# A new order of the FFN products, their sums, their weight buffers and the first loads in a two-layer trunk kernel

## The chip, the cores and the metric

The kernel runs on one core of a Trainium2 chip. The metric is device time in microseconds (us) of one execution. TensorE (PE) multiplies; VectorE (DVE), ScalarE (ACT) and GpSimd (POOL) do everything else on tiles of 128 partitions; SyncE (SP) only issues loads. Each engine works through its own list of instructions in order, and waits at an instruction until what that one needs has happened.

## The reference

Two layers, one sequence of 512 positions, width 1024, float32. Each layer is a mixer (layer 0: gated spatial mixing beside latent attention; layer 1: retention) and then a SwiGLU FFN of width 2816, each behind an RMSNorm and added to the residual `x`:

```
x = x + mixer(rmsnorm(x, g1))
h = rmsnorm(x, g2)
x = x + (silu(h @ w_gate) * (h @ w_up)) @ w_down      # 1024 -> 2816 -> 1024
```

The change touches the start of layer 0 and the two FFNs.

## The kernel before, in words

Activations are held transposed, in eight chunks of 128 features by 512 positions. A float32 product is three matmuls on a high and a low part of each side (hi·hi, hi·lo, lo·hi). Weights come as a "tape": `Tape.load` takes the next block of 128x1024 (512 KB), loads it over SP's queue into a buffer `w_raw` (L211), lets ACT round it to `w_hi` (L214) and DVE take the rest, `w_lo` (L215). Four blocks are kept split ahead of the product that uses them (DEPTH = 4). Activations are split the same way: `h_hi` by ACT (L356) and `h_lo` by DVE (L357) for the normed input, `a_hi` (L281) and `a_lo` (L282) for the FFN's inner values.

In the FFN the 22 blocks of 128 inner features are 11 pairs. Pair 0 is computed plainly ("whole"). Of each other pair, gate and up are got together by a Strassen-like scheme with seven products instead of eight. A product is 24 matmuls with a moving side of 256. Their names are A11, S1, S2, A12, S3, A22 and S4, after the weight blocks that they use. Three of the blocks are loaded plainly. S1 and S3 are sums of two blocks: a plain load (L211), then a second load on POOL's queue that adds into the same buffer (L213). S2 = A11 + S1 and S4 = A12 + S2 are made by DVE, in place in the first buffer (L199). S2, S3 and A22 go on accumulating in the PSUM bank `ps_x` that A11 began. Before each of S2, S3 and A22 starts, ACT has to copy the bank's state so far into a tile J: `take` (L894). `add` (L897, DVE) brings the other banks in. `finish` makes the inner values from a pair of rows: multiply by the norm's factor R (L877), Silu on ACT (L878), multiply by the other half (L879), split. After pairs 3, 7 and 10 the finished blocks go through w_down ("down", L923 and L924 add to `x`).

`ffn_steps` lists the products in the order in which TensorE does them. The order on the other engines is made by the tile framework's scheduler when the program is built; on the chip it is fixed. Loads of the tape wait until a buffer of the `raw` pool is free: 3 buffers in most of the kernel, 7 in the FFN.

Of the kernel before, what the change touches and what calls it, by code (L numbers as in the profile page):

```python
# [38 lines left out]
def ffn_steps():  # L39


    steps = [("whole", 0)]
    for p0, p1 in FF_PARTS:
        for p in range(max(p0, 1), p1):
            if p == 1:
                steps.append(("A11", p))
            steps += [("S1", p), ("S2", p), ("A12", p), ("S3", p)]
            if p + 1 < PAIRS:
                steps.append(("A11", p + 1))
            steps += [("A22", p), ("S4", p)]  # L50
        steps.append(("down", (p0, p1)))
    return steps


def tape_spec():

    out = []  # L60
    c = lambda a, n: np.arange(a, a + n)

    def load(name, k0, nk, cols, streams=False):
        key = (name, k0, int(cols[0]))
        block = (key, [(name, k0 + k, cols) for k in range(nk)], streams)
        out.append((key, ("load", block), nk, len(cols)))

    for m in range(2):
        load("even_w_in", 0, 8, c(1408 + 128 * m, 128))
    for m in range(3):  # L70
        load("even_w_in", 0, 8, c(1024 + 128 * m, 128))
    for k in range(0, 8, 2):
        load("even_w_in", k, 2, c(512, 512), True)
    head = np.arange(8)[:, None] * 128
    load("mla_w_ukv", 0, 2, (head + np.arange(64)[None]).ravel(), True)
    load("mla_w_ukv", 0, 2, (head + 64 + np.arange(64)[None]).ravel(), True)
    for k in range(3):
        load("mla_w_uq", k, 1, c(0, 768), True)
    for m in range(4):
        load("even_w_in", 0, 8, c(128 * m, 128))  # L80
    for k in (0, 4):
        for m in range(4):
            load("even_w_out", k, 4, c(256 * m, 256))

    def ffn(layer):
        gate, up, down = (f"ffn_w_{n}{layer}" for n in ("gate", "up", "down"))

        def block(i, j, p):

            cols = c(256 * p + 128 * i, 128)  # L90
            pieces = [(w, 2 * k + j, cols) for k in range(KD // 2) for w in (gate, up)]
            return ((gate, p, i, j), pieces, False)

        for name, p in ffn_steps():
            key = (layer, p, name)
            if name == "whole":
                for m in (2 * p, 2 * p + 1):
                    for w in (gate, up):
                        load(w, 0, 8, c(128 * m, 128))
                continue  # L100
            if name == "down":
                k0, k1 = 2 * p[0], 2 * p[1]
                for m in range(8):
                    load(down, k0, k1 - k0, c(128 * m, 128))
                continue
            how = {
                "A11": ("load", block(0, 0, p)),
                "A12": ("load", block(0, 1, p)),
                "A22": ("load", block(1, 1, p)),
                "S1": ("sum", block(1, 0, p), block(1, 1, p)),  # L110
                "S3": ("sum", block(1, 0, p), block(0, 0, p)),
                "S2": ("add", (layer, p, "A11"), (layer, p, "S1")),
                "S4": ("add", (layer, p, "A12"), (layer, p, "S2")),
            }[name]
            out.append((key, how, KD // 2, 256))

    def odd_out(h):
        for m in range(4):
            load("odd_w_out", 4 * h, 4, c(256 * m, 256))

    ffn(0)
    for h in range(RH):
        for base in (0, 1024):
            for m in range(2):
                load("odd_w_in", 0, 8, c(base + 256 * h + 128 * m, 128))
        for k in range(0, 8, 2):
            load("odd_w_in", k, 2, c(2048 + 512 * h, 512), True)
        for m in range(4):
            load("odd_w_in", 0, 8, c(4096 + 512 * h + 128 * m, 128))
        if h:  # L130
            odd_out(h - 1)
    odd_out(RH - 1)
    ffn(1)
    return out


def tape_blocks():

    blocks, at = {}, 0
    for _, how, _, _ in tape_spec():  # L140
        for b in how[1:] if how[0] != "add" else ():
            if b[0] not in blocks:
                blocks[b[0]] = (b, at)
                at += P * sum(len(cols) for _, _, cols in b[1])
    return blocks
# [31 lines left out]
class Tape:  # L177
# [13 lines left out]
    def load(self, pieces=1):  # L191
        key, how, nk, n = self.spec[len(self.made)]
        w = nk * n
        nc = self.nc
        hi = self.parts.tile([P, CHUNK], F32R, name="w_hi")
        lo = self.parts.tile([P, CHUNK], F32R, name="w_lo")
        if how[0] == "add":
            t = self.raws.pop(how[1])
            nc.vector.tensor_tensor(t[:, :w], t[:, :w], self.raws[how[2]][:, :w], op=ALU.add)  # L199
        else:  # L200
            t = self.raw.tile([P, CHUNK], F32, name="w_raw")
        self.raws[key] = t
        src = []
        if how[0] != "add":
            for b in how[1:]:
                at = self.begin[b[0]]
                src.append(self.wtape[at : at + P * w].rearrange("(p w) -> p w", p=P))
        for i in range(pieces):
            c = slice(i * w // pieces, (i + 1) * w // pieces)
            if src:  # L210
                nc.sync.dma_start(out=t[:, c], in_=src[0][:, c])  # L211
            for more in src[1:]:
                nc.gpsimd.dma_start(out=t[:, c], in_=more[:, c], accum_op=ALU.add)  # L213
            nc.scalar.copy(hi[:, c], t[:, c])  # L214
            nc.vector.tensor_tensor(  # L215
                lo[:, c], t[:, c], hi[:, c].bitcast(F32), op=ALU.subtract
            )
        view = lambda x: x[:, :w].rearrange("p (k n) -> p k n", k=nk)
        self.made.append((view(hi), view(lo)))

# [15 lines left out]
def trunk_kernel(ctx: ExitStack, tc: tile.TileContext, a: dict, out: bass.AP):  # L236
# [21 lines left out]
    def new_raw(stack, bufs):  # L258
        tape.raw = stack.enter_context(tc.tile_pool(name="raw", bufs=bufs))

    gains = const.tile([P, 4, KD], F32, name="gains")
    nc.scalar.dma_start(out=gains, in_=a["gains"])
    x = [res.tile([P, S], F32, name=f"x{k}") for k in range(KD)]
    ident = const.tile([P, P], F32, name="ident")
    make_identity(nc, ident)
    ones = const.tile([P, P], F32, name="ones")
    nc.vector.memset(ones, 1.0)
    mhalf = const.tile([P, 1], F32, name="mhalf")
    nc.vector.memset(mhalf, -0.5)
# [157 lines left out]
    with ExitStack() as e:  # L427
        new_raw(e, 3)
        h = []
        for k in range(KD):  # L430
            nc.sync.dma_start(out=x[k], in_=a["xT"][k * P : (k + 1) * P, :])
            if k == 0:
                tape.load(pieces=4)
            h.append(scaled_parts(0, k))
        tape.load(pieces=2)
        tape.ahead()
        new_tmp(e)
# [5 lines left out]
        for k in range(KD):  # L443
# [3 lines left out]
        cgain = ev.tile([P, 5], F32, name="cgain")  # L447
        qkg = ev.tile([P, 2, QK0], F32, name="qkg")
        rope0 = ea.tile([P, NT, 2, ROPE], F32, name="rope0")
        nc.gpsimd.dma_start(out=cgain, in_=a["lat_gT"])  # L450
        wk = ea.tile([P, KD, ROPE], F32, name="wk")
        nc.gpsimd.dma_start(out=wk, in_=a["kpe_w"])
        nc.gpsimd.dma_start(
            out=qkg, in_=a["qk_g"].rearrange("(o j) f -> o j f", o=1).broadcast_to([P, 2, QK0])
        )
        nc.gpsimd.dma_start(out=rope0, in_=a["rope0"])
        nc.gpsimd.dma_start(out=vgain, in_=a["gm_gT"])


        lat, latp = [], []  # L460
# [351 lines left out]
    def ffn(h, ss, which):  # L812
# [5 lines left out]


        with ExitStack() as e:  # L820
            new_raw(e, 7)
            fp = e.enter_context(tc.tile_pool(name="fp", bufs=1, reuse_waits="tile"))
            fp2 = e.enter_context(tc.tile_pool(name="fp2", bufs=2, reuse_waits="tile"))
            q = S // 2
# [109 lines left out]
            own = lambda t: t  # L934
            for name, p in ffn_steps():
                if name == "A11":
                    xs, rows = bank("ps_x"), [wide(), None]
                    products(xs, name, True)
                    take(rows[0], 0, xs)
                    following = (xs, rows)  # L940
                    if p == 1:
                        R = ss.rows(norm)
                        for m in range(2):
                            finish(m, undone(whole[m][0]), undone(whole[m][1]), plain)
# [7 lines left out]
                if name == "A12":  # L952
                    ws = bank("ps_w")
                    products(ws, name, True)
                    add(rows[0], 0, ws)
                if name == "S3":
                    products(xs, name, False)
                    rows[1] = wide()
                    take(rows[1], 1, xs, -1.0)
                    add(rows[1], 1, vs, ALU.subtract)  # L960
                    here = (xs, rows)
                if name == "A22":
                    xs, rows = here
                    products(xs, name, False)
                    take(rows[1], 0, xs, -1.0)
                    finish(2 * p + 1, rows[1][:, :S], rows[1][:, S:], own)
# [229 lines left out]
```

## Time and profile before

| | us |
|---|---|
| median of 3 runs (lowest, highest) | 1239.76 (1239.07, 1240.69) |
| the profiled execution | 1239.42 |
| its span, first to last instruction | 1237.6 |
| PE busy in the span | 1219.7 (99%) |
| DVE busy | 853.4 (69%) |
| ACT busy | 563.0 (45%) |
| POOL busy | 85.5 (7%) |
| mean granted TensorE clock | 0.997 |

PE, DVE, ACT and POOL are the compute engines; the busy time of PE is the sum of its matmuls, whose ends are modelled. What lies between the span and the execution's time, 1.8 us, is outside the program's instructions.

### The profile page before, as it was taken

The numbers are of one execution on the slowest core, as the hardware profiler recorded it, in microseconds if no ns is written. First come the engines' busy times: TensorE is split into PE (matmuls) and PEld (weight loads), VectorE is DVE, ScalarE is ACT, GpSimd is POOL, SyncE is SP. The second block draws the span as 40 slices with busy tenths as digits, with TensorE's granted clock in tenths as the row PEclk, the third lists the DMA queues.
The fourth block names the chain that finished last, engine by engine and source line by source line (L and its number), as shares of the span: only waits on it lengthen the run. The fifth ranks groups of instructions, "written<-read, shape, count | busy, mean of one in ns | idle before, by whom it ended". The sixth has DMA issues, their size and how long they took to land. (4 is left out here: it accounts for less than half of the span.)

```text
span 1237.6 us, 18425 instructions
## 1 busy us (share of the span) xinstructions
PE 1219.7 (99%) x7464; PEld 1106.2 (89%) x7464; DVE 853.4 (69%) x1226; ACT 563.0 (45%) x811; POOL 85.5 (7%) x89
## 2 busy tenths in 40 slices
PE   8999999999999999999999999999998999999998
PEld 6897778898999899888888888888888989998997
DVE  6597748986597577955474574574778756875774
ACT  5465746653366245534242242242466524652551
POOL 2062000100000000000000000000010000000000
PEclk9999999999999999999999999999999999999999
DMA  7223115655575556132231332332265565754631
GB/s 233 83 75 120 35 34 171 168 173 153 139 193 172 144 144 177 72 119 102 69 102 68 103 102 69 102 103 68 86 180 161 171 151 139 204 162 128 166 108 68
DMA packets 44980, 155.32 MB, mean 125 GB/s; under 512 B 5232, under 2 KB 5776, under 8 KB 44768
## 3 DMA queue, kind: packets, MB, share of 16 engines
q1 hardware_dynamic: 38304, 130.70, 31.7%
q0 software_dynamic: 6448, 23.45, 10.7%
q8 instruction: 58, 0.95, 0.3%
q14 instruction: 26, 0.21, 0.0%
q10 hardware_dynamic: 144, 0.02, 0.0%
HBM read 152.04 MB, written 2.10 MB: 125 GB/s over the span
## 5 line engine op out<-in xcount | busy, mean ns | idle before, releaser
L214 ACT CAST w_hi<-w_raw 128x1024 fp32r<-128x1024 f32 (+3 forms) x290 | 294.3, 1021 | 479.9 <-PE ps_mm L288 230.2
L215 DVE TENSOR_TENSOR w_lo<-w_raw,w_hi 128x1024 fp32r<-128x1024 f32 (+3 forms) x290 | 345.3, 1198 | 128.2 <-ACT w_hi L214 127.7
L287 PE MATMUL ps_mm<-h_hi,w_hi 128*128 128x512 f32 x456 | 175.4, 385 | 3.7 <-ACT h_hi L356 3.5
L288 PE MATMUL ps_mm<-h_lo,w_hi 128*128 128x512 f32 x456 | 173.9, 382 | 0.7 <-DVE h_lo L357 0.6
L289 PE MATMUL ps_mm<-h_hi,w_lo 128*128 128x512 f32 x456 | 173.5, 381 | 0.0
L865 PE MATMUL ps_x<-t_hi,w_hi 128*128 128x256 f32 x480 | 133.6, 278 | 6.7 <-ACT J L894 6.6
L287 PE MATMUL ps_mm<-a_hi,w_hi 128*128 128x512 f32 x352 | 133.5, 380 | 0.3 <-ACT a_hi L281 0.3
L289 PE MATMUL ps_mm<-a_hi,w_lo 128*128 128x512 f32 x352 | 133.6, 379 | 0.0
L288 PE MATMUL ps_mm<-a_lo,w_hi 128*128 128x512 f32 x352 | 133.6, 379 | 0.0
L865 PE MATMUL ps_x<-t_lo,w_hi 128*128 128x256 f32 x480 | 132.8, 277 | 0.0
L865 PE MATMUL ps_x<-t_hi,w_lo 128*128 128x256 f32 x480 | 132.8, 277 | 0.0
L287 PEld LDWEIGHTS ps_mm<-h_hi,w_hi 128*128 128x128 f32 x456 | 86.7, 190 | 16.5 <-ACT h_hi L356 3.8
L865 PEld LDWEIGHTS ps_x<-t_hi,w_hi 128*128 128x128 f32 x480 | 92.9, 194 | 8.2 <-ACT J L894 8.2
L288 PEld LDWEIGHTS ps_mm<-h_lo,w_hi 128*128 128x128 f32 x456 | 86.6, 190 | 14.2 <-DVE h_lo L357 2.4
L289 PEld LDWEIGHTS ps_mm<-h_hi,w_lo 128*128 128x128 f32 x456 | 86.6, 190 | 12.3 <-DVE w_lo L215 0.5
L865 PEld LDWEIGHTS ps_x<-t_lo,w_hi 128*128 128x128 f32 x480 | 92.9, 194 | 0.0
L865 PEld LDWEIGHTS ps_x<-t_hi,w_lo 128*128 128x128 f32 x480 | 92.9, 193 | 0.0
L213 POOL DMA_DIRECT2D w_raw<-in_wtape x40 | 34.7, 869 | 629.4 <-DMA w_raw<-in_wtape 249.2
L287 PEld LDWEIGHTS ps_mm<-a_hi,w_hi 128*128 128x128 f32 x352 | 66.5, 189 | 10.2 <-ACT a_hi L281 1.1
L289 PEld LDWEIGHTS ps_mm<-a_hi,w_lo 128*128 128x128 f32 x352 | 66.6, 189 | 9.3
L288 PEld LDWEIGHTS ps_mm<-a_lo,w_hi 128*128 128x128 f32 x352 | 66.7, 189 | 9.1
L923 DVE TENSOR_TENSOR t<-ps_mm,R 128x512 f32<-128x512 f32 x48 | 33.1, 689 | 59.3 <-PE ps_mm L289 59.2
(226 smaller groups left out, 2595.6 us busy)
## 6 DMA issues: line engine op xcount, KB each, us to landing
w_raw<-in_wtape SPq DMA_DIRECT2D x225, 512.0 KB, 3.5
w_raw<-in_wtape POOLq DMA_DIRECT2D x40, 512.0 KB, 5.8
w_raw<-in_wtape SPq DMA_DIRECT2D x19, 384.0 KB, 3.2
x<-in_xT SPq DMA_DIRECT2D x8, 256.0 KB, 6.4
out_T<-x SPq DMA_DIRECT2D x8, 256.0 KB, 2.0
decay<-in_decay POOLq DMA_DIRECT2D x1, 1024.0 KB, 7.2
w_raw<-in_wtape SPq DMA_DIRECT2D x4, 128.0 KB, 4.4
w_raw<-in_wtape SPq DMA_DIRECT2D x2, 256.0 KB, 6.2
```

Of the source, the lines that this page charges most:

```text
L213: nc.gpsimd.dma_start(out=t[:, c], in_=more[:, c], accum_op=ALU.add)
L214: nc.scalar.copy(hi[:, c], t[:, c])
L215: nc.vector.tensor_tensor(lo[:, c], t[:, c], hi[:, c].bitcast(F32), op=ALU.subtract)
L287: nc.tensor.matmul(acc, sh, mh, start=start, stop=False)
L288: nc.tensor.matmul(acc, sh, ml, start=False, stop=False)
L289: nc.tensor.matmul(acc, sl, mh, start=False, stop=stop)
L865: nc.tensor.matmul(o, s[:, k, cols], m, start=start and k + f + n == 0, stop=k == KD // 2 - 1 and n == 2, skip_group_check=True,)
L923: nc.vector.tensor_tensor(plain(t), undone(accs[j]), plain(R), op=ALU.mult)
```

## The change

First, the start. `x` comes as one tile laid out 128 x 8 x 512 and loaded by five DMAs (1, 1, 2, 2 and 2 chunks) where eight loaded one chunk each; the first weight block comes in two pieces instead of four. Five small loads (cgain, wk, qkg, rope0, vgain) go from POOL's queue to SP's, behind the first weight blocks. The names of these loads on SP's queue are those of the tiles; `x<-in_xP 128x1024` is two chunks. Before, rows of SP's order from its start:

```order
L431 DMA x_78<-in_xT 128x512
L211 DMA w_raw<-in_wtape 128x256 x4
L431 DMA x_79<-in_xT 128x512
L431 DMA x_80<-in_xT 128x512
L431 DMA x_81<-in_xT 128x512
L431 DMA x_82<-in_xT 128x512
L431 DMA x_83<-in_xT 128x512
L431 DMA x_84<-in_xT 128x512
L431 DMA x_85<-in_xT 128x512
L211 DMA w_raw<-in_wtape 128x512 x2
```

And now:

```order
L435 DMA x<-in_xP 128x512
L211 DMA w_raw<-in_wtape 128x512 x2
L435 DMA x<-in_xP 128x512
L435 DMA x<-in_xP 128x1024 x3
L211 DMA w_raw<-in_wtape 128x512 x2
L211 DMA w_raw<-in_wtape 128x1024 x2
L455 DMA cgain<-in_lat_gT 128x5
L457 DMA wk<-in_kpe_w 128x256
L458 DMA qkg<-in_qk_g 128x192
L461 DMA rope_211<-in_rope 128x256
L462 DMA vgain<-in_gm_gT 128x4
```

Nine loads stand ahead of the second weight block where twelve stood, and the small loads are on this queue.

Second, the FFN. A11 and A12 of the first pair come right after "whole", and within a pair the order is S1, S2, A11 of the next pair, S3, A12 of the next pair, A22, S4, where it was S1, S2, A12, S3, A11 of the next pair, A22, S4. The sum for S4 is made right behind the split of S2 (L220) and not when S4 is loaded. The raw pool has eight buffers instead of seven.

The scheduler's order on DVE moves with it. The place shown is one of those between two pairs: `t<-J,R` is L877 before and L882 now, `J<-J,ps_v` is the `add` that ends S4 of pair 4, and L199 is a sum of two weight buffers. The buffer on the left of the L199 rows holds A11 or A12; in brackets stands what a row waits for, DMASW being a load of POOL's queue. Before:

```order
L877 TENSOR_TENSOR t_3511<-J_3444,R_2316 128x512 [waits DVE_49,Activation_49]
L199 TENSOR_TENSOR w_raw_3521<-w_raw_3521,w_raw_3354 128x1024 [waits DVE_49]
L897 TENSOR_TENSOR J_2944<-J_2944,ps_v_3327 128x2x256 [waits PE_49]
L879 TENSOR_TENSOR t_3511<-t_3511,J_3444 128x512 [waits Activation_49]
L877 TENSOR_TENSOR t_3550<-J_2944,R_2316 128x512 [waits DVE_49]
L215 TENSOR_TENSOR w_lo_3559<-w_raw_3560,w_hi_3558 128x1024 [waits DMASW0_49]
L282 TENSOR_TENSOR a_lo1_3516<-t_3511,a_hi1_3515 128x512 [waits Activation_49]
L879 TENSOR_TENSOR t_3550<-t_3550,J_2944 128x512 [waits Activation_49]
L215 TENSOR_TENSOR w_lo_3591<-w_raw_3592,w_hi_3590 128x1024 [waits DMAHW3_49,PE_49]
L282 TENSOR_TENSOR a_lo0_3555<-t_3550,a_hi0_3554 128x512 [waits Activation_49]
L215 TENSOR_TENSOR w_lo_3622<-w_raw_3623,w_hi_3621 128x1024 [waits DMAHW4_49,PE_49,Activation_49]
L199 TENSOR_TENSOR w_raw_3592<-w_raw_3592,w_raw_3687 128x1024 [waits DMASW1_49,DVE_49]
```

And now:

```order
L882 TENSOR_TENSOR t_3528<-J_3461,R_2301 128x512 [waits DVE_49,Activation_49]
L199 TENSOR_TENSOR w_raw_3538<-w_raw_3538,w_raw_3704 128x1024 [waits DMASW4_49,DVE_49]
L902 TENSOR_TENSOR J_2897<-J_2897,ps_v_3344 128x2x256 [waits PE_49]
L884 TENSOR_TENSOR t_3528<-t_3528,J_3461 128x512 [waits Activation_49]
L882 TENSOR_TENSOR t_3567<-J_2897,R_2301 128x512 [waits DVE_49]
L215 TENSOR_TENSOR w_lo_3576<-w_raw_3577,w_hi_3575 128x1024 [waits DMASW3_49]
L286 TENSOR_TENSOR a_lo1_3533<-t_3528,a_hi1_3532 128x512 [waits Activation_49]
L884 TENSOR_TENSOR t_3567<-t_3567,J_2897 128x512 [waits Activation_49]
L215 TENSOR_TENSOR w_lo_3608<-w_raw_3609,w_hi_3607 128x1024 [waits DMAHW4_49,PE_49]
L286 TENSOR_TENSOR a_lo0_3572<-t_3567,a_hi0_3571 128x512 [waits Activation_49]
L215 TENSOR_TENSOR w_lo_3639<-w_raw_3640,w_hi_3638 128x1024 [waits DMAHW5_49,PE_49,Activation_49]
L220 TENSOR_TENSOR w_raw_3609<-w_raw_3609,w_raw_3538 128x1024 [waits DVE_49]
```

The second row was the sum for S4 of pair 5 (no load is waited for); now it is the sum for S2 of pair 6, whose second operand is the buffer that the load of POOL's queue adds into. Before, that sum was the last of the rows shown. The sum for S4 is now the last row (L220).

The diff, without what only renames:

```diff
-    steps = [("whole", 0)]
+    steps = [("whole", 0), ("A11", 1), ("A12", 1)]
     for p0, p1 in FF_PARTS:
         for p in range(max(p0, 1), p1):
-            if p == 1:
-                steps.append(("A11", p))
-            steps += [("S1", p), ("S2", p), ("A12", p), ("S3", p)]
-            if p + 1 < PAIRS:
-                steps.append(("A11", p + 1))
-            steps += [("A22", p), ("S4", p)]
+            following = [(n, p + 1) for n in ("A11", "A12") if p + 1 < PAIRS]
+            steps += [("S1", p), ("S2", p), *following[:1], ("S3", p)]
+            steps += [*following[1:], ("A22", p), ("S4", p)]
         steps.append(("down", (p0, p1)))
...
-                "S2": ("add", (layer, p, "A11"), (layer, p, "S1")),
-                "S4": ("add", (layer, p, "A12"), (layer, p, "S2")),
+                "S2": ("add", *((layer, p, n) for n in ("A11", "S1", "A12", "S4"))),
+                "S4": ("ready", (layer, p, "S4")),
...
-        if how[0] == "add":
+        if how[0] == "ready":
             t = self.raws.pop(how[1])
-            nc.vector.tensor_tensor(t[:, :w], t[:, :w], self.raws[how[2]][:, :w], op=ALU.add)
+        elif how[0] == "add":
+            t = self.raws.pop(how[1])
+            nc.vector.tensor_tensor(t[:, :w], t[:, :w], self.raws.pop(how[2])[:, :w], op=ALU.add)
         else:
             t = self.raw.tile([P, CHUNK], F32, name="w_raw")
-        self.raws[key] = t
+            self.raws[key] = t
...
+        if how[0] == "add":
+            sum4 = self.raws[how[4]] = self.raws.pop(how[3])
+            nc.vector.tensor_tensor(sum4[:, :w], sum4[:, :w], t[:, :w], op=ALU.add)
...
-    x = [res.tile([P, S], F32, name=f"x{k}") for k in range(KD)]
+    x_all = res.tile([P, KD, S], F32, name="x")
+    x = [x_all[:, k, :] for k in range(KD)]
...
-        for k in range(KD):
-            nc.sync.dma_start(out=x[k], in_=a["xT"][k * P : (k + 1) * P, :])
-            if k == 0:
-                tape.load(pieces=4)
-            h.append(scaled_parts(0, k))
+        for k0, k1 in ((0, 1), (1, 2), (2, 4), (4, 6), (6, 8)):
+            nc.sync.dma_start(out=x_all[:, k0:k1, :], in_=a["xP"][:, k0:k1, :])
+            if k0 == 0:
+                tape.load(pieces=2)
+            for k in range(k0, k1):
+                h.append(scaled_parts(0, k))
...
-        nc.gpsimd.dma_start(out=cgain, in_=a["lat_gT"])
+        nc.sync.dma_start(out=cgain, in_=a["lat_gT"])
...
-            new_raw(e, 7)
+            new_raw(e, 8)
...
                 if name == "A11":
-                    xs, rows = bank("ps_x"), [wide(), None]
-                    products(xs, name, True)
-                    take(rows[0], 0, xs)
-                    following = (xs, rows)
+                    following = (bank("ps_x"), [wide(), None])
+                    products(following[0], name, True)
+                    take(following[1][0], 0, following[0])
...
                 if name == "A12":
                     ws = bank("ps_w")
                     products(ws, name, True)
-                    add(rows[0], 0, ws)
+                    add(following[1][0], 0, ws)
```

## Rows read from the trace of the kernel before

**Rows 1.** The page: busy us, share of the span and instructions of each engine.

```profile
PE 1219.7 (99%) x7464; PEld 1106.2 (89%) x7464; DVE 853.4 (69%) x1226; ACT 563.0 (45%) x811; POOL 85.5 (7%) x89
```

**Rows 2.** Who PE waited for: us in total, times, longest us.

```profile
PE ps_x L865 <- ACT J L894: 6.6, 4, 2.8
PE ps_mm L287 <- ACT h_hi L356: 3.5, 1, 3.5
PE ps_v L865 <- DVE t_lo L282: 0.7, 2, 0.4
```

**Rows 3.** Stretches: length, busy us of each engine, granted clock, DMA share, GB/s.

```profile
10.78:14.20 3.42, 3.09 (x8) 2.07 (x7) 3.42 (x6) 3.42 (x7) 3.42 (x5) 0.50 1.05 392
939.20:942.60 3.40, 2.95 (x14) 2.96 (x15) 3.40 (x5) 1.33 (x2) 0.00 (x0) 0.50 0.62 117
```

**Rows 4.** DVE at the start: start, us, line, operation [idle before, releaser].

```profile
4.47 0.75 DVE L357 SCALAR_TENSOR_TENSOR h_lo<-x,gains,h_hi 128x512 fp32r<-128x512 f32 x1 [3.46 <-ACT h_hi L356]
5.14 0.42 DVE L215 TENSOR_TENSOR w_lo<-w_raw,w_hi 128x256 fp32r<-128x256 f32 x1
10.21 0.95 DVE L310 TENSOR_TENSOR ssum<-ssum,sq 128x512 f32<-128x512 f32 x1
11.08 1.53 DVE L357 SCALAR_TENSOR_TENSOR h_lo<-x,gains,h_hi 128x512 fp32r<-128x512 f32 x2
15.51 0.68 DVE L310 TENSOR_TENSOR ssum<-ssum,sq 128x512 f32<-128x512 f32 x1
16.11 0.74 DVE L357 SCALAR_TENSOR_TENSOR h_lo<-x,gains,h_hi 128x512 fp32r<-128x512 f32 x1
16.78 1.28 DVE L215 TENSOR_TENSOR w_lo<-w_raw,w_hi 128x512 fp32r<-128x512 f32 x2
```

**Rows 5.** ACT at the start: its wait for the second chunk of `x`.

```profile
8.79 0.72 ACT L356 ACTIVATE h_hi<-x,gains 128x512 fp32r<-128x512 f32 x1 [1.06 <-DMA x<-in_xT]
```

**Rows 6.** DMA issues at 0 to 8 us: KB each, median us to landing.

```profile
x<-in_xT SPq DMA_DIRECT2D x8, 256.0 KB, 6.4
rope<-in_rope POOLq DMA_DIRECT2D x1, 128.0 KB, 6.4
```

**Rows 7.** DVE between pairs 4 and 5 of the first FFN.

```profile
340.87 0.68 DVE L877 TENSOR_TENSOR t<-J,R 128x512 f32<-128x512 f32 x1
341.47 1.22 DVE L199 TENSOR_TENSOR w_raw<-w_raw 128x1024 f32<-128x1024 f32 x1
342.61 0.68 DVE L897 TENSOR_TENSOR J<-J,ps_v 128x512 f32<-128x512 f32 x1
```

**Rows 8.** The base load there, POOL's issue, and its time to landing (us, last).

```profile
332.98 0.33 SPq L211 DMA_DIRECT2D w_raw<-in_wtape  x1
337.84 0.87 POOL L213 DMA_DIRECT2D w_raw<-in_wtape  x1 [11.96 <-DMA w_raw<-in_wtape]
w_raw<-in_wtape POOLq DMA_DIRECT2D x1, 512.0 KB, 6.2
```

**Rows 9.** PE and ACT there: first matmul of S1, the take, first of S3.

```profile
341.24 0.28 PE L865 MATMUL ps_v<-t_hi,w_hi 128*128 128x256 f32 x1
348.34 0.59 ACT L894 ACTIVATE J<-ps_x 128x512 f32<-128x512 f32 x1
349.28 0.28 PE L865 MATMUL ps_x<-t_hi,w_hi 128*128 128x256 f32 x1
```

**Rows 10.** The first such place (pairs 1 and 2): DVE, POOL, landing.

```profile
243.75 1.22 DVE L199 TENSOR_TENSOR w_raw<-w_raw 128x1024 f32<-128x1024 f32 x1
241.79 0.87 POOL L213 DMA_DIRECT2D w_raw<-in_wtape  x1 [9.90 <-DMA w_raw<-in_wtape]
w_raw<-in_wtape POOLq DMA_DIRECT2D x1, 512.0 KB, 5.3
```

**Rows 11.** The last such place (second FFN, pairs 8 and 9).

```profile
1166.31 1.22 DVE L199 TENSOR_TENSOR w_raw<-w_raw 128x1024 f32<-128x1024 f32 x1
1162.51 0.86 POOL L213 DMA_DIRECT2D w_raw<-in_wtape  x1 [11.68 <-DMA w_raw<-in_wtape]
```

**Rows 12.** All L199 sums: what DVE waited for before them (us, times).

```profile
  DMA w_raw<-in_wtape: 18.3, 4
```

More of the change, by code (lines that the diff above doesn't have):

```diff
@@ L140, in tape_blocks @@
     for _, how, _, _ in tape_spec():
-        for b in how[1:] if how[0] != "add" else ():
+        for b in how[1:] if how[0] in ("load", "sum") else ():
             if b[0] not in blocks:
@@ L196, in load @@
         lo = self.parts.tile([P, CHUNK], F32R, name="w_lo")
-        if how[0] == "add":
+        if how[0] == "ready":
             t = self.raws.pop(how[1])
-            nc.vector.tensor_tensor(t[:, :w], t[:, :w], self.raws[how[2]][:, :w], op=ALU.add)
+        elif how[0] == "add":
+            t = self.raws.pop(how[1])
+            nc.vector.tensor_tensor(t[:, :w], t[:, :w], self.raws.pop(how[2])[:, :w], op=ALU.add)
         else:
             t = self.raw.tile([P, CHUNK], F32, name="w_raw")
-        self.raws[key] = t
+            self.raws[key] = t
         src = []
-        if how[0] != "add":
+        if how[0] in ("load", "sum"):
             for b in how[1:]:
@@ L262, in trunk_kernel @@
     nc.scalar.dma_start(out=gains, in_=a["gains"])
-    x = [res.tile([P, S], F32, name=f"x{k}") for k in range(KD)]
+    x_all = res.tile([P, KD, S], F32, name="x")
+    x = [x_all[:, k, :] for k in range(KD)]
     ident = const.tile([P, P], F32, name="ident")
     make_identity(nc, ident)
-    ones = const.tile([P, P], F32, name="ones")
+    ones = norm.tile([P, S], F32, name="sq", bufs=2)[:, :P]
     nc.vector.memset(ones, 1.0)
@@ L449, in trunk_kernel @@
         rope0 = ea.tile([P, NT, 2, ROPE], F32, name="rope0")
-        nc.gpsimd.dma_start(out=cgain, in_=a["lat_gT"])
+        nc.sync.dma_start(out=cgain, in_=a["lat_gT"])
         wk = ea.tile([P, KD, ROPE], F32, name="wk")
-        nc.gpsimd.dma_start(out=wk, in_=a["kpe_w"])
-        nc.gpsimd.dma_start(
+        nc.sync.dma_start(out=wk, in_=a["kpe_w"])
+        nc.sync.dma_start(
             out=qkg, in_=a["qk_g"].rearrange("(o j) f -> o j f", o=1).broadcast_to([P, 2, QK0])
         )
-        nc.gpsimd.dma_start(out=rope0, in_=a["rope0"])
-        nc.gpsimd.dma_start(out=vgain, in_=a["gm_gT"])
+        nc.sync.dma_start(out=rope0, in_=a["rope0"])
+        nc.sync.dma_start(out=vgain, in_=a["gm_gT"])
         lat, latp = [], []
@@ L960, in ffn @@
                     add(rows[1], 1, vs, ALU.subtract)
-                    here = (xs, rows)
                 if name == "A22":
-                    xs, rows = here
                     products(xs, name, False)
@@ L1172 @@
         "wtape": np.concatenate(pieces),
-        "xT": np.ascontiguousarray(w["x"][0].T),
+        "xP": w["x"][0].T.reshape(KD, P, S).transpose(1, 0, 2),
         "gains": np.stack([col(v) for v in (*w["norm_mix"], *w["norm_ffn"])], 1),
```

## The prediction

> **What bounds the kernel now.** I read the page's busy times first: PE is busy for 1219.7 of 1237.6 us, DVE for 853.4 [rows 1]. The change leaves every matmul in place, so it can only move what PE loses between matmuls. The list of PE's waits comes next. The reader is to see two places in it [rows 2]: one wait of 3.5 us for `h_hi` at the start, and four of together 6.6 us (longest 2.8) in which a product waits for `take`; 0.7 us of waits for `t_lo` stand beside them. These are the heads of the two FFNs. Third come the stretches with a lowered clock [rows 3]: 3.42 us at half speed in the start (10.78 to 14.20), and 3.40 us right behind the 2.8 us wait in the second FFN's head (939.2 to 942.6). Half speed costs half of such a stretch, 1.7 us. So the heads cost 6.6 + 0.7 + 1.7 = 9.0 us. Between the heads, the seven products of a pair follow each other without a gap: from S1 at 341.24 to S3 at 349.28 are three products in 8.04 us, 2.68 each [rows 9]. There DVE, ACT and the loads are hidden, and the question is by how much.
>
> **The start (x in five loads, small loads off POOL's queue).** The second chunk's `h_hi` starts at 8.79 and waited for `x` [rows 5]; the eight `x` loads of 256 KB take a median of 6.4 us to land, while a 128 KB load on POOL's queue takes 6.4 as well [rows 6]: they share the transfer engines. The Trainium skill (DMA: Bandwidth & Descriptors, "Queues, rings and completion order") says that each transfer engine serves the queues that have work for it in turn, a packet at a time; by that, small loads on another queue hold up `x`, and taking them away helps; the two 6.4 agree, though they are no proof.
>
> With `x` earlier, DVE sets the pace. It does the eight `h_lo`, the two halves of `w_lo` and three `ssum` before the last `h_lo` is done. I lay them end to end from the first `h_lo` at 4.47 [rows 4]: `h_lo` 0.67 (4.47 to 5.14), two `w_lo` of 0.64, then six more `h_lo` and three `ssum`. At the high prices (`h_lo` 0.72, half of 11.08 to 12.53; `ssum` 0.87, 10.21 to 11.08) the last `h_lo` starts at 4.47 + 0.67 + 1.28 + 6 x 0.72 + 3 x 0.87 = 13.4; at the low ones (0.67, and 0.60 from 15.51 to 16.11) at 12.2. Before it started at 16.11. That is 2.7 to 3.9 us; `x` may also land late: 2.5 MB at 295 to 392 GB/s are 6.5 to 8.5 us (392 in [rows 3]; the lower rate is my estimate, three quarters of it). I take 3.2 gained, with 1.5 and 4.5 as ends. The five small loads on SP's queue stand behind the weights and their users come later; I cost them at nothing, and at up to 0.5 if the next weight load queues behind them.
>
> **The heads (A11 and A12 of pair 1 behind "whole").** What PE waits for there is a chain on ACT and DVE whose length does not change. Before the first S2 stands one more product than before, so 2.68 us more of the chain are covered in each FFN [rows 9]. The four waits for `take` are 2.8 and three of together 3.8, 1.3 each [rows 2]; two of the three lie in the first FFN, 2.5 us, so about 0.2 stay. In the second 6.5 of the 9.0 us arise; 2.68 come off, and the wait that is left is too short to lower the clock if it behaves as the shorter ones of the list did, so 1.7 more: 2.1 stay, I take 2.3. Gain 9.0 - 2.5 = 6.5, ends 3 and 8.
>
> **The raw sums (S2 and S4 together).** Their number and length stay: 40 sums of 1.22 us [rows 7]. What moves is where they stand on DVE, and this decides the result. Between two pairs stands a chain that PE soon needs: `t<-J,R`, a sum (L199), `J<-J,ps_v`, then Silu and the splits, then on ACT, behind them in order, the `take` that frees `ps_x` for S3. Before, the sum in this slot was S4's, whose operands had long been there: DVE goes from 341.47 to 342.61 without a wait [rows 7]. Now it is the S2 sum of the pair after next, which needs what POOL's second load adds. In the trace that load is issued at 337.84 and lands 6.2 us later, at 344.04 [rows 8]; the slot comes at 341.47. DVE would stand for 2.6 us with everything behind it: the `add`, both halves of `finish`, the `w_lo` after them. Ahead of it the base load, issued at 332.98 [rows 8], has to land. It waits for a split, and in either program three more splits stand between that one and the slot, so eight buffers in place of seven don't bring it forward.
>
> The take ended at 348.93 and S3 began at 349.28 [rows 9]: 0.35 us of cover, the rest is PE's. There are eight such places (pairs 1, 4, 5 and 8 of each FFN; in the others a "down" stands between, which hides the wait, as it hides the four that DVE has now, 18.3 us in all [rows 12]). At the first the load lands at 241.79 + 5.3 = 247.1 for a slot at 243.75, 3.3 late [rows 10]; at the last at 1162.51 + 6.2 = 1168.7 for 1166.31, 2.4 late [rows 11]. The eight lie between 1.0 and 3.3 and sum to 18.0. Less 8 x 0.35 this is 15.2 us. The longest, about 2.95 after cover, is as long as the 2.8 that lowered the clock: 1.7 more. From below the bound is nothing (loads in time), from above 18.0 + three lowered clocks, 23. I take 15.2 + 1.7 = 16.9.
>
> The Trainium skill (same page, "Anatomy of one DMA") gives for a load of GpSimd's queue 2.0 us plus its bytes at 436 GB/s, an estimate of 3.2 us for 512 KB; by this the load of the example would land at 341.04, just before its slot, and the wait would vanish. The rows say 5.3 to 6.2, and they decide; this is the first rival.
>
> **Pair 10.** It has no next pair, so no product stands between its S2 and S3 now; the scheduler puts two matmuls of "down" there. At pair 5 the take ended 2.33 us after the end of S2 (346.60 by 2.68 a product). The sum of 1.14 us in the slot is absent before pair 10, so 1.2 us; the two matmuls cover some 0.4. About 0.8 in each FFN, 1.6, ends 0 and 4.6.
>
> **Sum.** Profiled execution 1239.4 (0.3 below the median, its span plus 1.8): - 3.2 - 6.5 + 16.9 + 1.6 = + 8.8, so 1248.2. I say 1248.
>
> **Rivals.**
> First: the second loads come in time. The order of the loads changes too, and POOL's load could land two or three us earlier relative to its slot; an eighth buffer, or a queue less full, would do it. For it: it needs only 1.0 to 3.3 us. Against it: the release of the base load stands where it stood, and the load on POOL's queue took 5.3 to 6.2 at each of these places. Then what is left is - 3.2 - 6.5 + 1.6: 1231.
>
> Second: the waits are there, but half of them is hidden or shorter than by these rows (PE arriving later gives the loads more time, and a stall at one place is time for the next load). Then 8 us of stalls: 1239.4 - 8.1 + 8 = 1239, anywhere from 1235 to 1242.
>
> Third, on the far side: each wait reaches PE in full and several lower the clock. Price 23 us in place of 16.9, and the head of the second FFN keeps its lowered clock, 1.7: 1256. It decides from the point where the waits exceed 2.8 us; [rows 10] is at 3.3.
>
> That the change does not do what it says I exclude for the order, which is fixed by the program; for the start it is possible: if transfers, not the small loads, hold `x`, the 3.2 shrink to 1.5, and the forecast goes to 1250.
>
> **How the numbers follow.** Forecast with its neighbours (1243 to 1253): 0.52. Third rival: 0.13. First: 0.20. Second: 0.15, of which a third is faster, a third the same, a third slower. A measurement of this kernel tells about 0.2%, 2.5 us, from no change. So faster 0.25, same 0.05, slower 0.70. The range reaches to the third rival above, 1256, and to 1234 below, which leaves out the better part of the first; the forecast's own range is 1243 to 1253.
>
> **What would show it.** Right: in the changed trace DVE idles some 2 us before L199 at eight places in pairs, put down to the load of `w_raw`, and PE's list shows as many waits of `ps_x` for J, about 2 us each, at S3; the waits at the FFN heads have nearly gone; the second chunk's `h_hi` comes before 7 us and the last `h_lo` at 12 to 13.5. Wrong: no idle time before L199 within the pairs, or idle time there with `ps_x` never waiting, or `x` still landing at 8 us and later.

## Result, and the profile after

The changed kernel takes 1259.9 us (median of 6 runs, 1257.77 to 1265.5) against 1239.66 us (6 runs, 1238.63 to 1240.69): ratio 1.0169, 95% interval 1.0147 to 1.0192, so 20 us slower. The forecast was 1248 and its range ended at 1256: the direction was right, the size was not. The profiled execution took 1262.88 us, 3 above the median, with a span of 1261.1; against [rows 1 to 3], whose span is 1237.6, 23.5 us have to be found.

PE's waits in the changed kernel, us in total, times, longest, beside [rows 2]:

```profile
PE ps_x L870 <- ACT J L899: 20.5, 10, 4.8
PE ps_v L870 <- ACT w_hi L214: 1.9, 1, 1.9
PE ps_mm L291 <- ACT w_hi L214: 1.7, 2, 0.9
PE ps_v L870 <- DVE w_lo L215: 1.0, 1, 1.0
PE ps_mm L291 <- ACT h_hi L360: 0.9, 1, 0.9
```

The wait for `take` has grown from 6.6 us in four to 20.5 us in ten. Eight of the ten are S3 within the pairs, where before there was none. The wait for `h_hi` at the start has shrunk from 3.5 to 0.9. What DVE waited for ahead of the sums of L199, beside [rows 12]:

```profile
  DMA w_raw<-in_wtape: 48.5, 14
```

The first place (pairs 1 and 2 of the first FFN; [rows 10] is the same place before): DVE, then POOL's two issues around it with the landing of the first, SP's two loads beside it with theirs, and last the `take` and S3's first matmul.

```profile
243.15 0.68 DVE L882 TENSOR_TENSOR t<-J,R 128x512 f32<-128x512 f32 x1
248.99 1.23 DVE L199 TENSOR_TENSOR w_raw<-w_raw 128x1024 f32<-128x1024 f32 x1 [5.16 <-DMA w_raw<-in_wtape]
250.13 0.68 DVE L902 TENSOR_TENSOR J<-J,ps_v 128x512 f32<-128x512 f32 x1
...
241.33 0.86 POOL L213 DMA_DIRECT2D w_raw<-in_wtape  x1 [10.91 <-DMA w_raw<-in_wtape]
w_raw<-in_wtape POOLq DMA_DIRECT2D x1, 512.0 KB, 7.6
...
237.91 0.33 SPq L211 DMA_DIRECT2D w_raw<-in_wtape  x1
w_raw<-in_wtape SPq DMA_DIRECT2D x1, 512.0 KB, 4.6
240.58 0.33 SPq L211 DMA_DIRECT2D w_raw<-in_wtape  x1
w_raw<-in_wtape SPq DMA_DIRECT2D x1, 512.0 KB, 5.5
...
255.86 0.59 ACT L899 ACTIVATE J<-ps_x 128x512 f32<-128x512 f32 x1
256.50 0.58 PE L870 MATMUL ps_x<-t_hi,w_hi 128*128 128x256 f32 x1 [4.78 <-ACT J L899]
```

The reader is to see the chain that the prediction drew: the sum stands in the slot, DVE is idle for 5.16 us until POOL's load has landed at 241.33 + 7.6 = 248.9, and S3 pays 4.78 of it. But the load took 7.6 us, not the 5.3 of [rows 10], although it was issued 0.46 us earlier. Two base loads ran beside it, until 242.5 and 246.1.

The eight waits are 5.16, 1.46, 4.40 and 1.86 us in the first FFN, 4.35, 0.98, 1.17 and 1.75 in the second, 21.1 in all. The rest of the 48.5 stands elsewhere: 9.9 before the very first sums of the two FFNs, 17.5 at four sums behind "down". The gaps before the eight S3, each the time between two matmul starts less their usual distance, sum to 19.5.

Stretches behind the three longest of them: length, busy us of each engine, granted clock, DMA share, GB/s.

```profile
256.30:259.75 3.45, 3.25 (x15) 3.25 (x16) 3.20 (x3) 1.58 (x3) 0.00 (x0) 0.51 0.42 140
379.20:386.05 6.85, 5.89 (x27) 5.89 (x28) 3.95 (x4) 2.87 (x5) 0.00 (x0) 0.50 0.51 168
980.00:983.40 3.40, 3.40 (x18) 3.40 (x17) 2.56 (x3) 0.94 (x2) 0.00 (x0) 0.50 0.45 155
```

After gaps of 4.95, 4.18 and 4.14 us PE runs for 13.7 us at 1.2 GHz instead of 2.4, which costs 6.8. The five gaps of 0.8 to 1.65 us lower nothing.

The account of the 23.5 us, from the two traces (both have 7464 matmuls, so the n-th of one can be set beside the n-th of the other): the start -1.4 (PE's 61st matmul, the warm-up's among them, at 18.34 and not 19.77); S3 within the pairs +19.5; lowered clock behind it +6.8; the heads -3.7 (1.3 in the first FFN, 2.4 in the second); pair 10 +2.4 (1.2 in each FFN). That sums to 23.6.

### The profile page after: what moved, and what is told of

Its sections match the earlier page's. It is cut to its first block, busy times and chain, and to the rows that moved or that the text cites. A ratio compares the mean times of both kernels' runs of the same rounds, so it can differ in the third digit from the quotient of the medians.

```text
span 1261.1 us, 18374 instructions
## 1 busy us (share of the span) xinstructions
PE 1228.0 (97%) x7464; PEld 1111.9 (88%) x7464; DVE 853.7 (68%) x1224; ACT 562.2 (45%) x809; POOL 83.6 (7%) x84
## 5 line engine op out<-in xcount | busy, mean ns | idle before, releaser
L214 ACT CAST w_hi<-w_raw 128x1024 fp32r<-128x1024 f32 (+2 forms) x288 | 293.6, 1027 | 484.8 <-PE ps_mm L292 231.0
L215 DVE TENSOR_TENSOR w_lo<-w_raw,w_hi 128x1024 fp32r<-128x1024 f32 (+2 forms) x288 | 344.1, 1204 | 125.3 <-ACT w_hi L214 124.8
L870 PE MATMUL ps_x<-t_hi,w_hi 128*128 128x256 f32 x480 | 136.2, 284 | 20.7 <-ACT J L899 20.5
L292 PEld LDWEIGHTS ps_mm<-h_lo,w_hi 128*128 128x128 f32 x456 | 86.8, 190 | 13.4 <-DVE h_lo L361 1.6
L291 PEld LDWEIGHTS ps_mm<-a_hi,w_hi 128*128 128x128 f32 x352 | 66.5, 189 | 12.2 <-ACT w_hi L214 2.1
```

The source lines that it names most:

```text
L215: nc.vector.tensor_tensor(lo[:, c], t[:, c], hi[:, c].bitcast(F32), op=ALU.subtract)
L291: nc.tensor.matmul(acc, sh, mh, start=start, stop=False)
L292: nc.tensor.matmul(acc, sh, ml, start=False, stop=False)
L870: nc.tensor.matmul(o, s[:, k, cols], m, start=start and k + f + n == 0, stop=k == KD // 2 - 1 and n == 2, skip_group_check=True,)
```

## Experiments

Each is compared with the kernel before, run on the same chip beside it; a ratio has its 95% interval.

**The sum behind the finish.** The edit tells the scheduler to keep eight S2 sums behind an instruction that is earlier in the program:

```diff
+            if self.behind is not None and key[1] in (3, 6, 7, 10):
+                self.tc.add_manual_dep(total.ins, self.behind.ins.name, ...)   # NoSync
...
-                split(hi, lo, t)
+                tape.behind = split(hi, lo, t)
```

> The changed kernel; the scheduler is told to put the S2 sum of pairs 3, 6, 7 and 10 on DVE behind the last a_lo of the finish of two pairs earlier, so out of the slot between t<-J,R and J<-J,ps_v. Nothing else moves. Theory (the wait of DVE in that slot is what costs): the eight waits before the sum (21.1 us in the changed kernel) vanish, with them the eight stalls of S3 (19.5 us) and the lowered clock behind four of them (about 6.8): 1260 - 26 = 1234 us, between 1231 and 1239. Rival (POOL's second loads are late for whoever needs them): DVE waits at the new place instead, S2's split or the next take comes late, and the time stays at 1250 or above.

Measured: 1236.72 us (11 runs) against 1240.2, ratio 0.9976 (0.9967 to 0.9985). DVE at the place shown above:

```profile
242.85 0.69 DVE L891 TENSOR_TENSOR t<-J,R 128x512 f32<-128x512 f32 x1
243.46 0.68 DVE L911 TENSOR_TENSOR J<-J,ps_v 128x512 f32<-128x512 f32 x1
...
248.26 1.28 DVE L295 TENSOR_TENSOR a_lo<-t,a_hi 128x512 fp32r<-128x512 f32 x2
249.46 1.22 DVE L200 TENSOR_TENSOR w_raw<-w_raw 128x1024 f32<-128x1024 f32 x1
```

and who PE waited for:

```profile
PE ps_v L879 <- ACT w_hi L222: 2.0, 1, 2.0
PE ps_mm L300 <- ACT w_hi L222: 1.7, 2, 0.9
PE ps_v L879 <- DVE w_lo L223: 1.4, 2, 1.0
...
PE ps_x L879 <- ACT J L908: 1.3, 1, 1.3
```

The `add` now follows `t` at once, the sum comes 6 us later and waits for nothing, and of the ten waits for `take` one is left. DVE's six other waits before sums (at the heads and behind "down", 28.6 us) stay. The order on DVE differs from the changed kernel's at these eight sums and at rows of the same `finish` that changed places with them, and nowhere else. So 23 us hung on the place of eight instructions among 1224. The theory holds; the rival falls. The time is 2.7 above the figure that I gave, within its range.

**Less of the load.** `S1`'s second load is cut to `slice(c.start, c.start + w // 4)`.

> The changed kernel in which S1's second load, on POOL's queue, adds only the first quarter of the block (128 of 512 KB; three quarters of that block are left out of the sum). The order on every engine is that of the changed kernel. Theory (the slot waits for this load to land, and its length is set by its bytes and by the base loads beside it): it lands some 2.5 us or more earlier, the eight waits of DVE (21.1 us) shrink to 5 or less, the stalls of S3 go with them and no clock is lowered behind them: 1235 to 1242. Rival (the length is a latency that bytes don't change, or the base load in front of it is what is late): waits and time stay, 1256 to 1264.

Measured: 1238.93 us (10 runs) against 1240.23, ratio 0.9995 (0.9982 to 1.0008). DVE's waits before L199:

```profile
  DMA w_raw<-in_wtape: 10.6, 5
  issue: 6.3, 3
```

From 48.5 us in 14 to 16.9 in 8, with the order on DVE untouched. The view puts three of these down to "issue", but each ends within 0.1 us behind the landing of POOL's load; two of them stand in the slot, 2.15 and 2.35 us at the first place of each FFN, here the first:

```profile
243.35 1.22 DVE L199 TENSOR_TENSOR w_raw<-w_raw 128x1024 f32<-128x1024 f32 x1 [2.15 <-issue]
```

So the eight waits shrank from 21.1 to 4.5. Two S3 still stalled, for 1.8 and 2.0 us, and the clock fell behind the second (959.3 to 962.7), which I had not expected. Taken with the run before: the sum in the slot and the landing of POOL's load are needed together; moving the first undoes the stalls, shortening the second nearly does.

**A load beside it.** In the kernel before, a load of 448 KB that nobody uses is issued on SP's queue as soon as S1's base block has landed.

```diff
+            if key[2:] == ("S1",):
+                extra = nc.sync.dma_start(out=self.beside, in_=src[0][:, :896])
+                self.tc.add_manual_dep(extra.ins, base.ins.name, ...)   # Sync: after base
```

> The kernel before with one more load: 448 KB on SP's queue, issued when S1's base block has landed, so beside S1's second load on POOL's queue; nothing uses it. Theory (a base load beside it lengthens a second load, as in the changed kernel at the three longest waits): S1's second loads that took 5.3 to 6.2 us take 7 or more. The time: DVE has some 8 us of room there, so 1240 to 1246. Rival (the second load's length does not depend on what runs beside it): it stays at 5.3 to 6.2.

Measured: 1241.46 us (8 runs) against 1239.87, ratio 1.0018 (1.0008 to 1.0028). The place of [rows 8], POOL's load and the load beside it with their times to landing:

```profile
340.77 0.86 POOL L213 DMA_DIRECT2D w_raw<-in_wtape  x1 [11.89 <-DMA w_raw<-in_wtape]
w_raw<-in_wtape POOLq DMA_DIRECT2D x1, 512.0 KB, 8.5
...
340.23 0.33 SPq L215 DMA_DIRECT2D beside<-in_wtape  x1
beside<-in_wtape SPq DMA_DIRECT2D x1, 448.0 KB, 5.4
```

6.2 us have become 8.5. At the eight places the load takes 6.9, 8.5, 6.3, 7.6, 7.5, 6.8, 7.6 and 7.7 us where it took 5.3, 6.2, 5.8, 5.8, 5.7, 5.3, 5.6 and 6.2; the median of all 40 goes from 5.8 to 7.2. So a load that runs beside lengthens POOL's, though three of the eight stay below the 7 that I expected. The kernel before hardly minds (1.6 us), since its sum comes late. The Trainium skill (DMA: Bandwidth & Descriptors, "Queues, rings and completion order") has the transfer engines serve the queues in turn; this run agrees in kind. The formula of its "Anatomy of one DMA" gives an estimate of 3.2 us for 512 KB; it held at no place, the shortest of the 40 taking 5.0.

**Seven buffers.** `new_raw(e, 7)` in the changed kernel.

> The changed kernel with seven raw buffers in the FFN instead of eight. The sum stands in the same slot on DVE. At three of the eight places POOL's second load took 7.6 us or so to land where it took 5.3 to 5.8 before the change. Theory (the eighth buffer lets a further base load run beside it): these land in 5.3 to 6.2 again, the eight waits sum to 15 to 18 us, and the time is about 1252. Rival 1 (the buffers have no part in it): 1257 to 1263. Rival 2 (with fewer buffers the base loads start later): over 1264.

Measured: 1279.56 us (4 runs), ratio 1.0323 (1.0309 to 1.0337). The time is the second rival's: DVE's waits before L199 are now

```profile
  DMA w_raw<-in_wtape: 77.7, 17
```

and at the first place DVE has

```profile
246.11 0.68 DVE L902 TENSOR_TENSOR J<-J,ps_v 128x512 f32<-128x512 f32 x1
253.84 1.22 DVE L199 TENSOR_TENSOR w_raw<-w_raw 128x1024 f32<-128x1024 f32 x1 [7.05 <-DMA w_raw<-in_wtape]
```

The sum did not stay in its slot: it stands one row later, behind the `add`, so the run changes more than the buffers. POOL's load is issued later too, here at 248.64, 1.9 us after DVE came to the sum, where in the changed kernel it was issued 2.5 us before. What my theory said of the load's length did come: at the three places of 7.3 to 7.6 us it took 5.1, 5.2 and 5.9, with one base load beside it that soon landed (within 2 us). The later issue cost more than that gave. The eighth buffer is worth some 20 us to the new order; by the program it holds an A12 that is loaded a pair ahead.

**S4's sum at its old time.** `"S4": ("add", (layer, p, "A12"), (layer, p, "S2"))` in place of `"ready"`.

> The changed kernel with the S4 sum made when S4 is loaded, as before the change; FFN order, eight buffers and start stay changed. Theory (the order of the products alone brings the S2 sum into the slot, since A11 of the next pair is loaded and split earlier relative to it): the waits stay, 1256 to 1264. Rival (the early S4 sum leaves the slot empty, and this lets the S2 sum in): the S4 sum stands in the slot again, no waits, 1233 to 1239.

Measured: 1265.74 us (4 runs, 1258.44 to 1267.55), ratio 1.0201 (1.0174 to 1.0228). In the trace, that of the fastest of the four, the S2 sum stands in the slot at all eight places and waits 17.4 us there; the first of them:

```profile
250.61 1.22 DVE L199 TENSOR_TENSOR w_raw<-w_raw 128x1024 f32<-128x1024 f32 x1 [5.28 <-DMA w_raw<-in_wtape]
```

So summing S4 along with S2 is not what hurts. The order of the products is: a run below with both sums at their old time, eight buffers and the old order within the pairs has no such wait.

**The start alone, and the small loads alone.** The first is the kernel before with all edits to the start, the second with the five `nc.sync.dma_start` for `nc.gpsimd.dma_start` and nothing else. Two things that the list of the change has wrong or leaves out belong here: seven loads, not nine, stand ahead of the second weight block (five of `x`, two of `w_raw`), and the start's edits also put `ones` into a buffer of the `sq` tiles.

> The kernel before with the changed start alone (x in one tile and five loads, first weight block in two pieces, small loads on SP's queue). Theory (the start gained the 1.4 us by which PE stands ahead in the changed trace from 20 us on, and nothing later depends on it): 1238.2, between 1237.6 and 1238.8. Rival (the 3.2 us of the forecast are there without the FFN's changes): 1236.5. Rival (no gain; the difference of one trace): 1239.7.

> The kernel before with the five small loads moved from POOL's queue to SP's and nothing else (x still in eight loads, first weight block in four pieces). Theory (the small loads held up x; the longer packets of x do little): the whole gain of the start alone, 1.5 to 2 us: 1238.2. Rival (x's layout brings it): no gain, 1240. Rival (both): about 1239.

Measured: the start 1238.14 us (11 runs), ratio 0.9986 (0.9977 to 0.9995); the small loads alone 1237.15 (11 runs), ratio 0.9977 (0.9968 to 0.9986). The gain is that of the small loads: alone they bring no less than all edits to the start. What the rest (x's longer packets, the first weight block's two pieces, `ones`) takes back, if anything, the two intervals leave open. In the run with the small loads alone the last `h_lo` starts at 14.06 (16.11 in [rows 4]):

```profile
8.28 0.75 DVE L357 SCALAR_TENSOR_TENSOR h_lo<-x,gains,h_hi 128x512 fp32r<-128x512 f32 x1 [1.09 <-ACT h_hi L356]
...
14.06 0.74 DVE L357 SCALAR_TENSOR_TENSOR h_lo<-x,gains,h_hi 128x512 fp32r<-128x512 f32 x1
```

**The new head with the old pairs, and eight buffers with the old order.**

> The changed start and eight buffers; A11 and A12 of pair 1 behind whole, but from pair 2 on the order of before within each pair, and both sums made at their own load as before, so that the S4 sum stands in the slot. Theory (the heads gain little; the rest of the new order only costs): no stall at S3 within the pairs, none before pair 10's S3; heads 5.3 us as in the run with the sum put behind, against 6.5 in the run with the start alone: 1237. Rival (the heads gain the 6.5 us of the forecast): 1232.

> The kernel before with the changed start and eight raw buffers in the FFN, order and sums as before. Theory (the order of before had its loads in time, so a further buffer brings nothing): 1238, as the start alone. Rival (eight buffers let the scheduler put an S2 sum ahead of what down's first product needs, which cost 8.8 us in the run with the new head): 1245 to 1248.

Measured: 1248.95 us (5 runs), ratio 1.0076 (1.0063 to 1.0089), and 1247.45 (10 runs, 1239.66 to 1254.22), ratio 1.0061 (1.0038 to 1.0085). The first I missed by 12 us. S3 doesn't wait in the pairs behind the first, but PE's longest wait is a new one in each, here in the first of the two:

```profile
PE ps_mm L291 <- DVE a_lo L285: 8.8, 3, 4.3
```

It stands at "down", where the S2 sum of the pair behind it comes on DVE ahead of the `a_lo` that down's first product needs:

```profile
997.27 1.22 DVE L201 TENSOR_TENSOR w_raw<-w_raw 128x1024 f32<-128x1024 f32 x1 [6.58 <-DMA w_raw<-in_wtape]
998.41 1.28 DVE L285 TENSOR_TENSOR a_lo<-t,a_hi 128x512 fp32r<-128x512 f32 x2
```

In the kernel before the same two stand the other way round, and so its four waits [rows 12] cost nothing. My expectation had left that out. It is the same pattern at another place, and the second run shows it without the new head (`a_lo`: 5.1 us, four times), so it comes with the eighth buffer and the old order.

**Pair 10.** On top of the first experiment, A12 of pair 10 stays between S2 and S3.

> The run with the S2 sum put behind, and in pair 10 A12 stays between S2 and S3 (its S4 sum is made when S4 is loaded). Theory (about 1.0 us is lost at S3 of pair 10 in each FFN, since nothing stands between S2 and S3 there): both go, 1236.7 - 2.0 = 1234.7. Rival (the take is late for another reason, or A12's place moves the stall on): 1236 to 1237.

Measured: 1235.0 us (5 runs) against 1240.23, ratio 0.9959 (0.9946 to 0.9972): 1.7 below the first experiment. The two waits for down's `w_hi`, 1.7 us, are gone.

**The best of them.** The same with x in eight loads again.

> The run with pair 10 restored, with x as before the change (eight loads, first weight block in four pieces) and only the small loads moved. Theory (the small loads bring 3 us and x's layout takes 1 back, independently of the FFN): 1235.0 - 1.0 = 1234.0. Rival (the start's gain differs from build to build and the layout does nothing): 1235.

Measured: 1234.8 us (5 runs) against 1239.87, ratio 0.9959 (0.9945 to 0.9972): 5 us faster than the kernel before and 25 faster than the changed one. 0.2 us from the run before is nearer the rival, that x's layout does nothing, but intervals of 1.6 us each way hold the theory's 1.0 too.

## Why the prediction was wrong

- **The mechanism** ("DVE would stand for 2.6 us with everything behind it", at eight places, paid by S3) was right, by the trace and by two experiments that take it away from either end, the first wholly, the second nearly.
- **The step that failed is the size of the term "raw sums", 16.9 us.** It measured 19.5 + 6.8 = 26.3: 4.3 more in gaps and 5.1 more in lowered clock. It took the landing of POOL's loads from the kernel before, 5.3 to 6.2 us. In the new order base loads are issued closer to them and run beside them: three of the eight took 7.3 to 7.6. Those are the three that made waits above 4 us, and the clock fell behind each of them; I had counted one lowered clock, 1.7 us. That a load beside it lengthens POOL's load the added load shows. That it was this at these three places rests on the traces: there a second base load was issued within 0.8 us of POOL's load, at the other five none was; and with seven buffers, without that second load, the three were short again. The forecast had named the loads' earlier landing as a rival, and had bounded the late side at 23 by lowered clocks alone, with the lengths of before. The cover of 0.35 us per place was also too much: 21.1 of waits left 19.5 of gaps, 0.2 each.
- **Luck**: the eight waits sum to 21.1, near the 18.0 forecast, because two errors cancel in part. At the three places they are 13.9 where the rows of before gave 6.4. At the other five POOL's load was issued 0.3 to 1.4 us further ahead of the slot than before, as the first rival had it, and they are 7.2 where the rows gave 11.7.
- **The heads** were put at 6.5 gained; 3.7 came. The first FFN's wait at S3 of pair 1 stayed at 1.5 (1.47 before): between S2 and S3 stands one product, as before, and my argument covered S2 only. In the second FFN S1 waits for its split (1.9 and 1.0). DVE idles 3.9 and 5.9 us before the very first sum of each FFN, which in the kernel before did not wait. The run with less of the load bears on this: there DVE idles 1.8 and 3.7 us, the wait at S3 of the first FFN is gone, and the heads gain 8.0 by the same count. So most of the loss hangs on the landing of POOL's loads there, which the forecast did not look at. That no clock fell in the second head came as forecast, but in the first experiment's trace it did fall there (931.0 to 934.4), behind waits of 1.95 and 0.96 us; those 1.7 us are not certain.
- **The start** was put at 3.2; in the changed kernel it gave 1.4, just under the lower of its ends. The step that failed is DVE's rows laid end to end: DVE stood 1.06 us for the third chunk's `h_hi`, which started only at 8.73 after a wait for `x`, and the last `h_lo` comes at about 14.0, not at 12.2 to 13.4. The two waits, and the changed kernel's loads of x by the page, KB each and median us to landing:

```profile
8.73 1.33 ACT L360 ACTIVATE h_hi<-x,gains 128x512 fp32r<-128x512 f32 x2 [1.17 <-DMA x<-in_xP]
9.48 1.41 DVE L361 SCALAR_TENSOR_TENSOR h_lo<-x,gains,h_hi 128x512 fp32r<-128x512 f32 x2 [1.06 <-ACT h_hi L360]
...
x<-in_xP SPq DMA_DIRECT2D x3, 512.0 KB, 6.9
x<-in_xP SPq DMA_DIRECT2D x2, 256.0 KB, 3.6
```

  The pairing of chunks in loads of 512 KB does not by itself explain the 14.0: with x in eight loads, in the run with the small loads alone, DVE waits 1.09 us at the second chunk instead and the last `h_lo` starts at 14.06. Nor had the forecast a term for the clock: the half speed at the start is still in the changed kernel's trace (10.6 to 14.0) and not in those of the start alone and the small loads alone, in which PE stands 1.6 and 2.0 us ahead.
- **Pair 10** was put at 1.6 and measured 2.4; the experiment gave 1.7 back. The wait that PE shows there is not the forecast's late take but `w_hi` of down's block, 0.85 us in each FFN; the take ended only at 500.07, just before S3 at 500.16, so without that wait it would have held S3 as long.
- The sum failed at its upper end because all four terms missed in the same direction, by 9.4, 2.8, 1.8 and 0.8 us. The far-side rival, 1256, had the right mechanism and too few of its effects.

## What to carry to other kernels

An in-order engine makes an instruction that waits for a load into a wait of all that stands behind it; so read for each such instruction not whether its own result is needed soon, but what is queued behind it. When a change of order moves loads closer together, the time to landing of before is no measure of after: take the longest that the trace shows with two loads in flight. Here the trace of before had it: four of POOL's loads outside the heads took 6.9 to 8.0 us, each with an SP load issued within 0.3 us of it. The place that a scheduler picks for an instruction can be corrected with one dependency. And more buffers are no safe gain: the eighth was worth 20 us to the new order and cost the old one some 8.

## What the runs showed of the hardware

How long a load of 512 KB on POOL's queue takes that adds into its target goes with how near to it SP issues a load. In the traces before and after, the heads of the FFNs left out, it took 6.8 to 8.0 us in the eleven cases with an SP load issued within 0.6 us of it, 5.4 to 7.6 in the fifteen with one within 0.6 to 1 us (the first place, 7.6, among them), and 5.2 to 5.9 in most of those with none within 1 us (three took 6.2 to 6.7, and two right behind another load of POOL's queue 7.8 and 8.7).

TensorE's granted clock, in the FFNs, went to half behind gaps of 4.1 us and more in the changed kernel and behind the wait of 2.8 us in the kernel before; in these two traces it did not behind gaps of up to 2.1 us. But a short gap is no guarantee. In the run with the start alone, whose FFNs are those of the kernel before, it fell behind the second FFN's first wait for `take`, 1.26 us; behind the same wait, 1.25 us, it stayed at full speed in the kernel before. The matmul that waited and the stretch behind it (length, busy us of each engine, granted clock, DMA share, GB/s), first the start alone, then the kernel before:

```profile
929.45 0.46 PE L867 MATMUL ps_x<-t_hi,w_hi 128*128 128x256 f32 x1 [1.26 <-ACT J L896]
929.65:933.00 3.35, 3.35 (x17) 3.35 (x17) 3.35 (x4) 0.61 (x2) 0.00 (x0) 0.50 0.30 103
...
931.25 0.38 PE L865 MATMUL ps_x<-t_hi,w_hi 128*128 128x256 f32 x1 [1.25 <-ACT J L894]
931.30:934.70 3.40, 3.40 (x31) 3.40 (x31) 3.37 (x5) 0.65 (x2) 0.00 (x0) 1.00 0.31 89
```

So the length of a wait alone does not tell whether the clock falls behind it.
